# A second Strassen level for one more product of an MLP kernel, with its sums chained through ScalarE and its weights split on VectorE

## The chip, the cores and the metric

The kernel runs on one core of a Trainium2 chip. The metric is device time in microseconds (us) of that core. A run over 1.5% above the fastest of its kernel would count as slow. The engines are PE (TensorE), DVE (VectorE), ACT (ScalarE), POOL (GpSimd) and SP (SyncE, which here only issues DMAs).

## The reference

```python
x: (8, 1024, 1024)   w1: (1024, 4096)   w2: (4096, 1024)      # float32
h = x @ w1
h = 0.5 * h * (1 + np.tanh(np.sqrt(2 / np.pi) * (h + 0.044715 * h ** 3)))
return (h @ w2).astype(np.float32)
```

## The kernel before

The 8192 rows of x go through in eight superblocks of 1024 rows, SB0 to SB7. Both matmuls of a superblock use one Strassen level: seven products M1 to M7 of half-size blocks instead of eight. The first matmul works through sixteen chunks of the hidden dimension; `g` is the result after the activation, as four blocks `g["11"]` to `g["22"]` in SBUF. From SB2 on, the second matmul applies the scheme once more inside M1, M2, M3, M6 and M7 (class `Inner`, seven inner products each), and M4 and M5 are plain.

An inner product needs sums of w2's sub-blocks ("splits"), which are made once from w2's blocks (the "raw pieces", loaded from DRAM), written to DRAM and loaded again in every superblock. The splits of M1 and M3 are made on GpSimd in SB2's first matmul. At the end of every first matmul from SB2 on, GpSimd also makes four differences of g's sub-blocks in advance (`EARLY`).

```python
# in matmul1, for each chunk c of 16; product() is 4 matmuls of 512 columns on PE; banks from 8 of PSUM
product(pb, w, 4, True, False);  v = temp();  nc.scalar.copy(out=v, in_=pb)
product(qb, w, 5, True, False);  u = temp();  tt(u, v, qb, SUB)      # SBUF tensor and PSUM bank
...                                                                 # four more tt of that kind
if sb == 2 and c < 8 and c % 2 == 0:
    split_on_pool(FROM_SUMS[c // 4], c // 2 % 2)                    # GpSimd: w2 splits of M1, M3
...
if sb > 1 and c >= NI - 4:                                          # GpSimd: the early differences
    m, b = EARLY[c - NI + 4]
    early[m][b] = unit(NI // 2, HT // 2)
    gu, gv = (inner_block(g[t], b) for t in A_TERMS[m])
    nc.gpsimd.tensor_tensor(out=early[m][b], in0=gu, in1=gv, op=SUB)

# matmul2: Inner.steps, cut; three PSUM banks, evacuated by ScalarE twice and by VectorE otherwise
self.multiply(1, ab, True);   v = temp(); act_copy(v, ab)
self.multiply(6, bb, True);   tt(c12, pair(v), pair(bb), ADD, True)
self.multiply(2, ab, False);  act_copy(c11, pair(ab))
...
```

`tt` is a `tensor_tensor` on VectorE, `unit` a 4 KB-per-partition buffer from a pool of 26, `True` as its last argument pins its place in the engine's order. Such a pinned operation holds up everything behind it in VectorE's queue (in the changed kernel, behind a pair of splits that takes 9.73 us from 483.97, the next sum starts at 493.62, though PE had stopped at 487.64).

## Time and profile before

| | before |
|---|---|
| median | 1527.61 us (three runs, 1527.45 to 1528.31) |
| span of the profiled run | 1525.9 us |
| PE busy | 1517.1 us, 99% |
| one first matmul | 96.8 us |
| plain product M4 or M5 | 13.81 us |
| second-level product | 12.23 us |

The head of the profile page, kernel before (busy time, share of the span, instructions):

```profile
span 1525.9 us, 22990 instructions
PE 1517.1 (99%) x8702; PEld 852.3 (56%) x8702; DVE 1073.8 (70%) x1354; ACT 486.3 (32%) x817; POOL 357.2 (23%) x380
```

PE is busy all the time, so the time is the sum of the matmuls. The timeline of PE, kernel before, SB2's second matmul (columns: start, duration, engine, line, operation, output<-input, shape, count; a bracket at the end, where there is one, gives idle time ahead and what ended it):

```profile
505.86 13.98 PE L791 MATMUL ps<-u,g 128*128 128x512 f16 x64
519.67 1.91 PE L726 MATMUL ps<-u 128*128 128x256 f16 x16
...
556.36 13.98 PE L791 MATMUL ps<-u,gc 128*128 128x512 f16 x64
570.17 1.91 PE L726 MATMUL ps<-u,g 128*128 128x256 f16 x16
```

M4 runs from 505.86 to 519.67, M5 from 556.36 to 570.17: 13.81 us each. M1, M2 and M3 fill the 36.69 us between 519.67 and 556.36, 12.23 us each. No line has a bracket: nothing waits.

In the opening, VectorE makes sums of two SBUF tensors (`u<-u`, 128x2048 f16) while GpSimd casts weights. The timelines of VectorE and of GpSimd, kernel before:

```profile
114.39 1.22 DVE L142 TENSOR_TENSOR u<-u 128x2048 f16<-128x2048 f16 x1
116.12 0.68 DVE L142 TENSOR_TENSOR tmp<-tmp,ps 128x512 f32<-128x512 f32 x1
116.72 1.85 DVE L142 TENSOR_TENSOR u<-u 128x2048 f16<-128x2048 f16 x1
```

```profile
114.93 2.56 POOL L161 CAST u<-gc 128x1024 f16<-128x1024 f32 x2 [3.07 <-PE ps L366]
```

The same operation takes 1.22 us at 114.39, where it starts ahead of the casts, and 1.85 us at 116.72, where a cast of GpSimd, the second of the pair, still runs until 117.49. The first cast of the pair, which started behind VectorE's operation at 114.39, was held in its turn: it lasted 1.57 us, where most of the 30 casts of this shape in the trace last 1.04. The operation with a PSUM operand keeps its 0.68 us beside a cast.

### The profile page before, as it was taken

The page shows a single profiled execution, that of the slowest core. Times are in us where ns is not written, and L with a number is a line of the kernel's source. Part 1 is how long each engine was busy: PE and PEld are TensorE (multiplying, and loading weights), DVE is VectorE, ACT ScalarE, POOL GpSimd, SP SyncE. Part 2 cuts the span into 40 slices and gives each one's busy share as a digit, 9 for nine tenths or more (in the row PEclk, how much of TensorE's full clock was granted, in tenths as well). Part 3 has the DMA queues.
Part 4 walks back from the last instruction along what each step waited for, and adds up shares of the span by engine and source line. Part 5 has one row for each costly group of instructions (what it writes and reads, how often), then busy time and mean ns, then how long its engine had stood idle before and what let it go on. Part 6 is the DMA issues. An engine that isn't in the chain of part 4 may idle for free.

```text
span 1525.9 us, 22990 instructions
## 1 busy us (share of the span) xinstructions
PE 1517.1 (99%) x8702; PEld 852.3 (56%) x8702; DVE 1073.8 (70%) x1354; ACT 486.3 (32%) x817; POOL 357.2 (23%) x380
## 2 busy tenths in 40 slices
PE   9999999999999999999999999999999999999999
PEld 4444444444444677446764477544875448744486
DVE  5876868768755787557875587656876567855786
ACT  6655024410144212442124411344113441144300
POOL 1242011211297022130212203131121400204011
PEclk9999999999999999999999999999999999999999
DMA  9999985894998899769996699966999769993697
GB/s 317 348 327 349 253 281 184 281 304 156 351 362 232 309 324 312 240 159 328 321 305 212 176 348 320 312 186 198 329 308 325 185 211 320 306 353 90 221 326 185
DMA packets 226191, 417.84 MB, mean 274 GB/s; under 512 B 78752, under 2 KB 85920, under 8 KB 225184
## 3 DMA queue, kind: packets, MB, share of 16 engines
q1 hardware_dynamic: 193536, 314.64, 61.4%
q0 software_dynamic: 32544, 101.73, 24.4%
q8 instruction: 68, 1.11, 0.3%
q14 instruction: 43, 0.35, 0.1%
HBM read 311.43 MB, written 119.54 MB: 282 GB/s over the span
## 4 chain that ended last, share of the span: by engine, by line
PE 85%; DVE 0%; issue 0%
PE ps L366 44%; PE ps L726 24%; PE ps L791 17%; DVE u L142 0%
## 5 line engine op out<-in xcount | busy, mean ns | idle before, releaser
L366 PE MATMUL ps<-u 128*128 128x512 f16 x3584 | 776.1, 379 | 3.6 <-DVE tmp L142 1.5
L366 PEld LDWEIGHTS <-u 128*128 128x128 f16 x3584 | 350.5, 98 | 427.1 <-issue 4.7
L142 DVE TENSOR_TENSOR tmp<-tmp,ps 128x512 f32<-128x512 f32 x528 | 361.7, 686 | 298.1 <-ACT tmp L430 114.6
L376 ACT ACTIVATE g<-tmp 128x512 f16<-128x512 f32 x256 | 161.1, 630 | 294.4 <-DVE tmp L142 294.3
L726 PE MATMUL ps<-u,gc 128*128 128x256 f16 x1920 | 224.3, 273 | 0.0
L142 DVE TENSOR_TENSOR u<-u 128x2048 f16<-128x2048 f16 (+3 forms) x233 | 211.9, 937 | 16.6 <-ACT u L321 11.7
L791 PE MATMUL ps<-u,gc 128*128 128x512 f16 x1024 | 222.6, 379 | 0.0
L726 PEld LDWEIGHTS <-gc 128*128 128x128 f16 x1920 | 187.9, 98 | 21.7
L376 ACT ACTIVATE g<-ps 128x512 f16<-128x512 f32 x256 | 151.4, 596 | 88.1 <-PE ps L366 87.9
L791 PEld LDWEIGHTS <-gc 128*128 128x128 f16 x1024 | 100.1, 98 | 119.6
L791 PE MATMUL ps<-u,g 128*128 128x512 f16 x640 | 139.8, 379 | 0.0
L490 POOL DMA_DIRECT2D out_dram<-u x58 | 58.5, 1019 | 311.2 <-DVE u L142 299.0
L142 DVE TENSOR_TENSOR u<-u,ps 128x512 f32<-128x512 f32 x131 | 89.7, 685 | 46.1 <-PE ps L791 17.0
L158 ACT COPY tmp<-ps 128x512 f32<-128x512 f32 x54 | 31.6, 585 | 272.1 <-PE ps L726 161.3
L469 POOL TENSOR_TENSOR u<-g,g 128x2048 f16<-128x2048 f16 x24 | 97.2, 4067 | 75.0 <-ACT g L376 60.1
L791 PEld LDWEIGHTS <-g 128*128 128x128 f16 x640 | 62.7, 98 | 75.5
L726 PE MATMUL ps<-u,g 128*128 128x256 f16 x864 | 103.1, 273 | 0.0
L478 POOL DMA_DIRECT2D out_dram<-u x52 | 39.0, 770 | 249.0 <-ACT u L158 227.3
L430 ACT COPY tmp<-ps 128x512 f32<-128x512 f32 x128 | 72.9, 569 | 69.7 <-PE ps L366 69.7
L142 DVE TENSOR_TENSOR tmp<-ps,tmp 128x512 f32<-128x512 f32 x128 | 88.3, 690 | 5.9 <-PE ps L366 1.2
L726 PEld LDWEIGHTS <-g 128*128 128x128 f16 x864 | 84.5, 98 | 11.1
L142 DVE TENSOR_TENSOR u<-tmp,ps 128x512 f32<-128x512 f32 x60 | 41.3, 688 | 63.9 <-PE ps L726 41.4
(42 smaller groups left out, 736.2 us busy)
## 6 DMA issues: line engine op xcount, KB each, us to landing
u<-w_d SPq DMA_DIRECT2D x384, 256.0 KB, 7.2
u<-in_d SPq DMA_DIRECT2D x120, 512.0 KB, 7.3
u<-raw_d SPq DMA_DIRECT2D x132, 256.0 KB, 6.6
out_dram<-u POOLq DMA_DIRECT2D x58, 512.0 KB, 9.0
u<-raw_d SPq DMA_DIRECT2D x56, 512.0 KB, 7.1
gc<-in_w_dram SPq DMA_DIRECT2D x48, 512.0 KB, 6.5
w_d<-u POOLq DMA_DIRECT2D x36, 512.0 KB, 4.2
raw_d<-u SPq DMA_DIRECT2D x32, 512.0 KB, 9.9
```

The costliest lines, as they stand in the source:

```text
L142: i = nc.vector.tensor_tensor(out=out, in0=in0, in1=in1, op=op)
L158: tc.keep_in_program_order(nc.scalar.copy(out=out, in_=in_))
L366: nc.tensor.matmul(bank, lhsT=ops[:, k, :], rhs=xs[m][:, k, :], start=(first and k == 0), stop=(k == KH - 1), skip_group_check=not first,)
L376: gelu_last[0] = nc.scalar.activation(out=g[b][:, c, :], in_=src, func=GELU)
L430: nc.scalar.copy(out=v, in_=pb)
L469: nc.gpsimd.tensor_tensor(out=early[m][b], in0=gu, in1=gv, op=SUB)
L478: return nc.gpsimd.dma_start(out=out2[r0:r0 + P, o0:o0 + OH], in_=src, **kw)
L490: return nc.gpsimd.dma_start(out=rows, in_=src, **kw)
L726: tc.keep_in_program_order(nc.tensor.matmul(bank[:, i * OH // 2:(i + 1) * OH // 2], lhsT=t[:, c, i * P:(i + 1) * P], rhs=self.y[j][:, c, : ...
L791: i = nc.tensor.matmul(pair(bank), lhsT=a[:, c, :], rhs=chunks(pieces[c // QC])[:, :, c % QC, :], start=(first and c == 0), stop=(c == NI ...
```

## The change

Its intent: give M5 the second level too (1.58 us less of PE time in each of SB2 to SB7), let one PSUM bank keep accumulating through four of the seven inner products while ScalarE copies its running value out, which relieves VectorE, and make M5's w2 splits in SB2's first matmul beside those of M1 and M3. M1's stay on GpSimd; M3's and M5's go to VectorE, two operations each in chunks 5 to 12. GpSimd's early differences become six.

```diff
-FROM_SUMS = (1, 3)
-INNER = MADE_INNER + FROM_2 + FROM_SUMS
+IN_M1 = {0: (1, 0), 1: (1, 1), 2: (5, 0), 3: (3, 0), 5: (3, 1), 7: (5, 1)}
+INNER = MADE_INNER + FROM_2 + (1, 3, 5)
-EARLY = ((1, "11"), (1, "21"), (2, "11"), (2, "21"))
-W_ORDER = (1, 6, 2, 7, 5, 4, 3)
+EARLY = ((1, "11"), (1, "21"), (2, "11"), (2, "21"), (6, "11"), (6, "21"))
+W_ORDER = (1, 2, 6, 5, 7, 3, 4)
 ...
-            if sb == 2 and c < 8 and c % 2 == 0:
-                split_on_pool(FROM_SUMS[c // 4], c // 2 % 2)
+            if sb == 2:
+                if c in IN_M1:
+                    jobs = split_in_m1(*IN_M1[c])
+                    while jobs and c < 2:
+                        jobs.pop(0)()                    # M1: on GpSimd, at once
+                    splits += jobs
+                for _ in range(2 if 4 < c < 13 else 0):
+                    splits.pop(0)()                      # M3, M5: on VectorE, pinned
 ...
+            if sb == 2 and c == NI - len(EARLY):
+                mark = nc.gpsimd.tensor_copy(out=pace, in_=g["11"][:, c, :2])
-            if sb > 1 and c >= NI - 4:
+            if sb > 1 and c >= NI - len(EARLY):
 ...                                                     # in Inner.steps, a is kept accumulating:
+            for n, (j, bank, first, out, adds) in enumerate((
+                (1, a, True, "11", ()),
+                (2, b, True, None, ("11",)),
+                (6, a, False, "12", ()),
+                (5, c, True, None, ("12",)),
+                (7, a, False, "22", (("22", c),)),
+                (3, b, True, None, ("12",)),
+                (4, a, False, "21", ()),
+            ), 1):
+                self.multiply(j, bank, first)
+                if out is not None:
+                    t = quarter(into, out)
+                    if self.base is None:
+                        act_copy(t, pair(bank))
 ...                                                     # load(): the two result halves ("into") of a
+            into = dict(zip((2, 5), into))               # product are taken from the pool of units
+                if j in into:                            # after its second and its fourth weight tile
+                    into[j]()
```

(Cut: `W_SUMS` and the job table of the second matmul are rewritten, the next superblock's x differences partly go in place.)

## The prediction

> **What bounds the kernel now.** TensorE. The profile's first part gives PE 1517.1 of 1525.9 us (99%) busy; in the timeline nothing waits after the first 45 us, and PE's waits sum to under 5 us. Granted clock 0.999. So time is the sum of matmuls. From differences of starts in the timeline (busy spans overlap): a plain product of the second matmul (64 matmuls of 512 columns) takes 13.81 us, 215.8 ns each; a second-level product (7 x 16 matmuls of 256 columns) 12.23 us, 109.2 ns each. [...]
>
> **Removed.** M5's 64 wide matmuls become 112 narrow ones in six superblocks (SB2 to SB7): 13.81 - 12.23 = 1.58 us each, 9.5 us in all (0.62%), all on the critical path if nothing new stalls PE. Also gone: M5's accumulating store into block 12.
>
> **Added.**
> - VectorE, per superblock: M5's differences and sums (8 of 1.22 us) replace 4 of 1.22; more f32 adds of 0.685 us to fold M5 in; one evacuating add less in each inner product (ScalarE copies instead, 0.585 us); two differences move to GpSimd (4.07 us each, late in the first matmul). Second matmul before: about 41 x 1.22 + 41 x 0.685 = 78 of 88.7 us; after: 43 x 1.22 + 44 x 0.685 = 82.6 of 87.2 us, 95%. I estimate M6 overbooked (14 us in 12.2), a lag of about 3 us that the next stage absorbs.
> - DMA, per superblock: 1.5 MB more w2 loads, 1 MB fewer stores. The windows by stage show DMA share 0.95 to 1.08 and 253 to 374 GB/s, so it is near full; but by the order of SP's queue loads are free to issue at least 14 us before use (18 before the change), against 7 to 8 us to landing.
> - PSUM: the bank that keeps accumulating must be copied by ScalarE (0.585 us) while one other 16-matmul product (1.75 us) runs: fits.
> - SB2 only: 4 MB more traffic in a first matmul at 0.92 DMA share (340 to 409 GB/s early), with a quiet stretch (103 to 142 GB/s, 481 to 493 us) to absorb it; 16 VectorE operations of 0.72 us in slots where VectorE is busy 3.4 of 6 us. Fits.
> - SB7: M7 evacuates by VectorE, behind M6's lag: I estimate 0.5 to 1 us of PE wait, once.
>
> **Predicted.** 1527.6 - 9.5 + about 1 = 1519.0 us; 80% range 1517.4 to 1522.5. Faster by over 2%: 0.01; within 2%: 0.97; slower by over 2%: 0.02.
>
> **What would show it.** Right: PE 99% and continuous; M5's stage 12.2 instead of 13.8 us, a superblock 183.9 instead of 185.5; SB2's first matmul still 97 us; 288 more matmuls; VectorE over 90% in the second matmul; DMA share about 1.0 in M3, which had 253 GB/s. Wrong: PE idle at M6 or M7 released by a DMA (all 26 buffers used) or by VectorE (lag over 4 us, last sums late); PE idle at the third or fifth product inside an inner product, released by ScalarE.
>
> **What would make it wrong.** Sustained DMA saturation from M3 to M7, with loads landing after 14 us rather than 8: some us per superblock, which would eat the gain. VectorE's lag compounding (its waits for banks and the four sum buffers leave no slack). In SB2, raw pieces landing late would block VectorE's in-order queue, and with it the first matmul.

## The result, and the profile after

Slower: 1550.41 us median (1549.01 to 1552.05, four runs) against 1527.96 (1527.45 to 1528.82), ratio 1.0147 (95% interval 1.0129 to 1.0164). A ratio is the mean time of one kernel's fast runs over that of the other's of the same rounds, so it is not quite the ratio of the medians quoted.

The head of the page and two of its groups, kernel after (a group's columns: line, engine, operation, output<-input, shape, count | busy us, mean ns of one | idle us just before them, and what ended most of it):

```profile
span 1548.7 us, 23813 instructions
PE 1515.2 (98%) x8990; PEld 881.3 (57%) x8990; DVE 1127.1 (73%) x1400; ACT 520.1 (34%) x874; POOL 370.2 (24%) x359
...
L367 PE MATMUL ps<-u 128*128 128x512 f16 x3584 | 782.0, 381 | 19.8 <-DVE tmp L143 18.3
...
L750 PE MATMUL ps<-u,gc 128*128 128x256 f16 x2304 | 257.5, 273 | 7.7 <-ACT u L159 7.5
```

There are 288 more matmuls, as intended, but PE now waits: 18.3 us in the first matmuls for VectorE (16.8 of them in SB2's), and 7.5 us in second-level products for ScalarE. Where, the timeline of PE tells, kernel after:

```profile
450.89 1.02 PE L367 MATMUL ps<-u 128*128 128x512 f16 x4 [1.26 <-DVE tmp L143]
...
494.35 8.76 PE L367 MATMUL ps<-u 128*128 128x512 f16 x28 [6.71 <-DVE tmp L143]
511.43 17.39 PE L367 MATMUL ps<-u 128*128 128x512 f16 x68 [8.32 <-DVE tmp L143]
...
752.61 3.66 PE L750 MATMUL ps<-u,g 128*128 128x256 f16 x32
756.94 7.15 PE L750 MATMUL ps<-u,gc 128*128 128x256 f16 x64 [0.67 <-ACT u L159]
...
765.67 3.66 PE L750 MATMUL ps<-u 128*128 128x256 f16 x32
770.16 7.15 PE L750 MATMUL ps<-u,gc 128*128 128x256 f16 x64 [0.84 <-ACT u L159]
```

The first three lines are SB2's first matmul, the last four M3 and M5 of SB3. The windows of two stages, kernel after: SB2's first matmul, then SB3's M1 to M7 without M4 (columns: window, length, then for PE, PEld, DVE, ACT and POOL busy us and instructions, granted clock of PE, DMA share, GB/s):

```profile
409.27:528.65 119.38, 102.60 (x449) 45.04 (x448) 88.20 (x100) 45.49 (x78) 61.64 (x55) 0.93 0.88 282
...
728.16:803.35 75.19, 73.68 (x674) 65.74 (x672) 62.97 (x76) 14.07 (x24) 9.84 (x11) 1.00 0.96 301
```

And the same two in the kernel before, SB2's first matmul and M1 to M7 without M4 of SB3:

```profile
409.04:505.86 96.82, 96.82 (x449) 43.82 (x448) 57.35 (x84) 45.70 (x78) 65.55 (x52) 1.00 0.92 298
...
705.13:780.07 74.94, 74.94 (x625) 61.08 (x624) 59.85 (x71) 8.79 (x15) 14.59 (x18) 1.00 1.02 321
```

So there are two losses.

- **SB2's first matmul** takes 119.4 us, and 96.8 before: 22.6 us more.
- **Each of SB2 to SB6** should save 1.58 us in the second matmul. SB3's goes from 74.94 to 75.19 us, because M3 takes 13.06 and M5 13.22 us instead of 12.23: 0.83 + 0.99, about 1.83 us lost (the run bufs below was forecast with 1.84). SB7 has neither wait.

The sum: -6 x 1.58 + 22.6 + 5 x 1.83 = +22.3 us. Measured, the medians differ by 22.45 us.

What VectorE and GpSimd did in SB2's last chunks, the timelines of VectorE and of GpSimd, kernel after:

```profile
477.92 1.29 DVE L143 TENSOR_TENSOR u<-u 128x1024 f16<-128x1024 f16 x2
...
483.97 9.73 DVE L143 TENSOR_TENSOR gc<-gc 128x1024 f16<-128x1024 f16 x2
...
498.56 12.22 DVE L143 TENSOR_TENSOR gc<-gc 128x1024 f16<-128x1024 f16 x2
```

```profile
484.35 8.06 POOL L479 TENSOR_TENSOR u<-g,g 128x2048 f16<-128x2048 f16 x2
...
497.55 4.07 POOL L479 TENSOR_TENSOR u<-g,g 128x2048 f16<-128x2048 f16 x1
501.56 8.05 POOL L479 TENSOR_TENSOR g<-g,g 128x2048 f16<-128x2048 f16 x2
```

The two splits of chunk 10 took 1.29 us together. Those of chunk 11 took 9.73 us, and those of chunk 12 12.22 us, and each pair ends just after GpSimd's early differences end (484.35 + 8.06 = 492.41, VectorE 493.70; 501.56 + 8.05 = 509.61, VectorE 510.78). The trace counts VectorE as busy all the while, so no wait is listed for these splits. Behind them in VectorE's queue stand the sums that free PSUM's banks, and PE stops.

PE also loses more than it waits for. The windows around the wait of 6.71 us, kernel after (the last three columns are granted clock, DMA share, GB/s):

```profile
490.00:493.00 3.00, 0.00 (x0) 0.00 (x0) 2.97 (x1) 0.00 (x0) 2.41 (x1) 0.96 1.33 262
493.00:496.00 3.00, 1.65 (x4) 0.55 (x4) 2.48 (x4) 1.07 (x2) 0.00 (x0) 0.50 0.57 126
496.00:499.00 3.00, 3.00 (x9) 1.03 (x8) 1.73 (x3) 0.97 (x3) 2.55 (x3) 0.50 0.72 199
```

After the idle time the granted clock is 0.50, and matmuls start 0.427 us apart instead of 0.216: about seven in 3 us where fourteen start at full clock (a window also counts those that only reach into it). In this trace the clock fell 5.1 and 3.3 us after PE had stopped, and came back 5.2 us after PE had started again, both times. (Shorter waits, in two runs below, differ: in the run both one of 1.90 us, with one of 0.17 after it, was followed by a clock of 0.50 in the window 454 to 456 us; four waits in M4 of the run later, 1.76 us the longest, were not, with 1.00 in the windows from 505 to 514 us.) SB2's first matmul lost 22.6 us, with 16.8 us of waits; of the rest, 5.8 us, about 5.1 is this clock (26 matmuls in all that started later than at full clock).

### The profile page after: what moved, and what is told of

Its sections match the earlier page's. It is cut to its first block, busy times and chain, and to the rows that moved or that the text cites. A ratio compares the mean times of both kernels' runs of the same rounds, so it can differ in the third digit from the quotient of the medians.

```text
span 1548.7 us, 23813 instructions
## 1 busy us (share of the span) xinstructions
PE 1515.2 (98%) x8990; PEld 881.3 (57%) x8990; DVE 1127.1 (73%) x1400; ACT 520.1 (34%) x874; POOL 370.2 (24%) x359
## 4 chain that ended last, share of the span: by engine, by line
PE 82%; DVE 2%; issue 1%; ACT 0%; DVEq 0%; ACTq 0%
PE ps L367 43%; PE ps L750 28%; PE ps L801 12%; DVE gc L143 1%; DVE u L143 1%; ACT u L159 0%; DVE g L143 0%; DVE tmp L143 0%; DVEq L143 0%; ACTq L159 0%
## 5 line engine op out<-in xcount | busy, mean ns | idle before, releaser
L367 PE MATMUL ps<-u 128*128 128x512 f16 x3584 | 782.0, 381 | 19.8 <-DVE tmp L143 18.3
L367 PEld LDWEIGHTS <-u 128*128 128x128 f16 x3584 | 351.9, 98 | 447.8 <-issue 28.7
L750 PE MATMUL ps<-u,gc 128*128 128x256 f16 x2304 | 257.5, 273 | 7.7 <-ACT u L159 7.5
L143 DVE TENSOR_TENSOR u<-u 128x512 f32<-128x512 f32 (+3 forms) x286 | 245.6, 892 | 16.4 <-ACT u L322 12.5
L159 ACT COPY u<-ps 128x512 f32<-128x512 f32 x164 | 96.1, 586 | 419.2 <-PE ps L750 300.4
L500 POOL DMA_DIRECT2D out_dram<-u x68 | 66.6, 1177 | 404.1 <-DVE u L143 355.5
L143 DVE TENSOR_TENSOR u<-u,ps 128x512 f32<-128x512 f32 x164 | 111.9, 682 | 41.0 <-PE ps L801 16.1
L801 PE MATMUL ps<-u,gc 128*128 128x512 f16 x640 | 138.8, 379 | 0.0
L750 PE MATMUL ps<-u 128*128 128x256 f16 x864 | 99.2, 273 | 0.0
L750 PEld LDWEIGHTS <-u 128*128 128x128 f16 x864 | 84.5, 98 | 11.1
L143 DVE TENSOR_TENSOR u<-g,g 128x2048 f16<-128x2048 f16 x48 | 57.5, 1220 | 44.2 <-PE ps L750 40.0
```

The costliest lines, as they stand in the source:

```text
L143: i = nc.vector.tensor_tensor(out=out, in0=in0, in1=in1, op=op)
L159: tc.keep_in_program_order(nc.scalar.copy(out=out, in_=in_))
L367: nc.tensor.matmul(bank, lhsT=ops[:, k, :], rhs=xs[m][:, k, :], start=(first and k == 0), stop=(k == KH - 1), skip_group_check=not first,)
L500: return nc.gpsimd.dma_start(out=rows, in_=src, **kw)
L750: tc.keep_in_program_order(nc.tensor.matmul(bank[:, i * OH // 2:(i + 1) * OH // 2], lhsT=t[:, c, i * P:(i + 1) * P], rhs=self.y[j][:, c, : ...
L801: i = nc.tensor.matmul(pair(bank), lhsT=a[:, c, :], rhs=chunks(pieces[c // QC])[:, :, c % QC, :], start=(first and c == 0), stop=(c == NI ...
```

## The experiments

Theory 1 for the first loss: VectorE's splits read two SBUF tensors, and such an operation cannot run while GpSimd runs one of its own, but waits (the lock, below). VectorE's sums in the first matmul read one SBUF tensor and one PSUM bank and are free of it. The trace before fits both halves (1.85 instead of 1.22 us, and 0.68 us kept, beside a cast); port, lock and free test them. Rivals: GpSimd only shares bandwidth; the slots are too full for VectorE; the raw pieces come late by DMA.

Theory B for the second loss: ScalarE's copy waits for its target buffer, not for its input. In the built program's addresses, the target of the first copy of M3 (`into[3]`) has the slot that M3's own second weight tile leaves, so it can't be written before the second inner product is done. That of M5 has the slot of M2's result, which VectorE is still adding up. Building the kernel again and matching its instructions with the trace confirms both: in SB3 the last matmul that reads that weight tile ends at 756.27 and the copy starts at 756.31; VectorE's last addition on M2's result ends at 769.45 and the copy starts at 769.53. Rival: ScalarE or VectorE is late by itself.

### port: the lock by itself

A kernel of its own (it returns zeros). Its output is wrong, which doesn't matter for the time. Each phase is meant to start both engines together:

```python
def v_two16(): nc.vector.tensor_tensor(out=vo, in0=va, in1=vb, op=SUB)   # 128x1024 f16, two SBUF tensors
def v_psum():  nc.vector.tensor_tensor(out=fo, in0=fa, in1=ps, op=SUB)   # 128x512 f32, SBUF and PSUM
def v_copy32(): nc.vector.tensor_copy(out=fo, in_=fa)                    # 128x512 f32, one SBUF tensor
def g_two():   nc.gpsimd.tensor_tensor(out=go, in0=ga, in1=gb, op=SUB)   # 128x2048 f16
def g_dma():   nc.gpsimd.dma_start(out=out2[r:r + P, :], in_=zero)
phase(v_two16, 6, None, 0);  phase(v_two16, 6, g_two, 3);  phase(v_psum, 8, g_two, 3)
...                                              # two-input f32, and one-input copies, f16 and f32
phase(v_two16, 6, g_copy, 3);  phase(v_two16, 12, g_dma, 6)
```

> The disputed cost by itself; the result is zeros on purpose, so wrong. Phases: VectorE operations of one kind, alone or while GpSimd runs three tensor_tensor of 128x2048 f16 back to back (about 12 us). Theory 1 (a VectorE operation that reads two SBUF tensors cannot run while GpSimd runs one, and waits, counted as busy, until GpSimd is done): two-input f16 operations take 0.68 us alone, but the one that meets GpSimd lasts until GpSimd's last of the three ends (8 us or more); those that read one SBUF tensor and PSUM keep 0.69 us. Theory 2 (GpSimd merely shares bandwidth): all of them longer by some tens of per cent, none by many us. Theory 3 (the long operations of the changed kernel waited for late DMA data or buffers): nothing is longer here, since no DMA is in these phases. For two-input f32, for one-input copies and for GpSimd issuing DMAs I have no firm expectation; they are measured to learn.

Measured, the timelines of VectorE and then of GpSimd, run port:

```profile
7.26 4.32 DVE L119 TENSOR_TENSOR vo<-va,vb 128x1024 f16<-128x1024 f16 x6
...
11.96 15.63 DVE L119 TENSOR_TENSOR vo<-va,vb 128x1024 f16<-128x1024 f16 x6
...
31.88 5.73 DVE L125 TENSOR_TENSOR fo<-fa,ps 128x512 f32<-128x512 f32 x8
...
75.11 10.17 DVE L131 COPY fo<-fa 128x512 f32<-128x512 f32 x6
...
95.28 8.68 DVE L119 TENSOR_TENSOR vo<-va,vb 128x1024 f16<-128x1024 f16 x12
```

```profile
11.90 12.97 POOL L134 TENSOR_TENSOR go<-ga,gb 128x2048 f16<-128x2048 f16 x3
...
27.89 12.33 POOL L134 TENSOR_TENSOR go<-ga,gb 128x2048 f16<-128x2048 f16 x3
...
95.11 3.33 POOL L141 DMA_DIRECT2D out_dram<-zero  x6
```

Six two-input operations take 4.32 us alone (0.72 each) and 15.63 us beside three of GpSimd: one by one, the first three lasted 4.55, 4.42 and 4.42 us, the next three 0.69. Eight operations with a PSUM operand ran beside the second and third of GpSimd's (32.02 to 40.22 us) at 0.69 us each; the first of the three had already held a small copy of VectorE that prepares the phase (3.99 us). GpSimd issuing DMAs held nothing up here: twelve take 8.68 us (0.72 each). A one-input copy between SBUF tensors was held too (0.43 us alone, 4.15 beside GpSimd). Theory 1 stands in its main point, and bandwidth sharing falls. Late data falls as a necessary cause, since no operand here comes by DMA. (My text said that no DMA is in these phases. The writing of the zeros to DRAM in fact ran beside them until about 78 us, and the first and the third phase were none the longer for it. Between 85 and 95 us, where the DMA share is 0.00, a two-input operation beside a one-input copy of GpSimd still took 2.26 us instead of 0.69.) One part of what I expected was off: each waiting operation got in after one operation of GpSimd, not after all three. Here GpSimd left a gap of 0.08 us between its operations; in the changed kernel they followed without one, and a split waited for two or three of them. The gap is not shown to be what decides: in the run lock below GpSimd left none, and VectorE got in after one (2.08 and 4.42 us for the pair at 655.06).

### apart, bufs, both: each cause taken away, and the two together

apart keeps VectorE's splits as they are and moves GpSimd's work in SB2:

```diff
-            if sb == 2 and c == NI - len(EARLY):
-                mark = nc.gpsimd.tensor_copy(out=pace, in_=g["11"][:, c, :2])
 ...                                   # cut: other superblocks keep one difference a chunk from chunk 10
+            if sb == 2:
+                if c == 13:
+                    mark = nc.gpsimd.tensor_copy(out=pace, in_=g["11"][:, c, :2])
+                pick = {13: EARLY[:1], 14: EARLY[1:2], 15: EARLY[2:4]}.get(c, ())
 ...                                   # cut: M6's two in SB2, by VectorE in M4
```

> The changed kernel, with one thing moved in SB2: GpSimd's early differences start after chunk 13 (not 10), after VectorE's last w2 split, and are four (not six; the two of M6 are made by VectorE in M4 as in the kernel before). VectorE's splits stay as they are. Theory 1 (lockout by GpSimd): SB2's first matmul falls from 119.4 to 97 to 99 us, no split over 2 us but the one in chunk 5 that meets the end of GpSimd's M1 splits; time 1550.4 - 21 = about 1529 to 1531. Rival (slots too full for VectorE, or raw pieces late by DMA): the splits in chunks 11 and 12 still stall, time stays about 1548 to 1551.

bufs is one line:

```diff
-    up = ctx.enter_context(tc.tile_pool(name="up", bufs=26))
-    tp = ctx.enter_context(tc.tile_pool(name="tp", bufs=10))
+    up = ctx.enter_context(tc.tile_pool(name="up", bufs=27))
+    tp = ctx.enter_context(tc.tile_pool(name="tp", bufs=9))
```

> The changed kernel with 27 instead of 26 buffers in the pool of units (and 9 instead of 10 of temporaries, to make room). In SB2 to SB6 the changed kernel loses 1.84 us at the third product of M3 and of M5, where PE waits for ScalarE's copy. Theory B (the copy waits for its target: the slot that the pool gave it still holds M3's own second weight tile, or M2's sums): with 27 buffers the copy runs 1.75 us sooner, a steady superblock falls from 185.7 to about 183.9 us, time 1550.4 - 5 x 1.84 = 1541.2, SB2's first matmul still 119. Rival (ScalarE or VectorE is late by itself): no change, 1550.

both has the two edits.

> Both edits: what the prediction had expected of the change. If the two causes are all there is: 1527.9 - 9.5 = about 1518.4 plus up to 2 us, and so 0.6% under the kernel before. If something else holds it, above 1522.

Measured, all correct, three rounds beside the kernel before (1528.44 us):

| run | median | ratio to before | SB2's first matmul | a steady superblock |
|---|---|---|---|---|
| changed kernel (its own rounds) | 1550.41 | 1.0147 | 119.4 | 185.7 |
| apart | 1531.9 (1527.92 to 1532.68) | 1.0023 | 97.2 | 185.7 |
| bufs | 1542.15 (1539.91 to 1544.18) | 1.0088 | 117.7 | 183.87 |
| both | 1522.7 (1521.49 to 1523.24) | 0.996 | 100.8 | 183.87 |

The two columns on the right are from the profiled runs. In apart the two splits that had lasted 9.73 and 12.22 us last 1.41 and 1.29, timeline of VectorE:

```profile
481.60 1.41 DVE L143 TENSOR_TENSOR gc<-gc 128x1024 f16<-128x1024 f16 x2
487.64 1.29 DVE L143 TENSOR_TENSOR gc<-gc 128x1024 f16<-128x1024 f16 x2
```

They stand in the same slots, with the same raw pieces from DRAM, so neither the slots nor the DMA were the cause. In bufs the copy in M3 comes when its bank is done. The timeline of ScalarE around the first copy of SB3's M3, first in the kernel after (where M3 begins at 752.61), then in bufs (where it begins at 749.17); the first line of each is the last copy of M2, and the third line of the first is M5's first copy (M5 begins at 765.67):

```profile
752.81 0.59 ACT L159 COPY u<-ps 128x512 f32<-128x512 f32 x1 [2.91 <-PE ps L750]
756.31 0.59 ACT L159 COPY u<-ps 128x512 f32<-128x512 f32 x1 [2.91 <-PE ps L750]
...
769.53 0.59 ACT L159 COPY u<-ps 128x512 f32<-128x512 f32 x1 [3.07 <-DVE u L143]
```

```profile
749.37 0.59 ACT L159 COPY u<-ps 128x512 f32<-128x512 f32 x1 [2.91 <-PE ps L750]
751.12 0.59 ACT L159 COPY u<-ps 128x512 f32<-128x512 f32 x1 [1.16 <-PE ps L750]
```

M3's first copy (756.31 and 751.12) comes 3.70 us after M3's beginning in the first, when two inner products are done, and 1.95 us in the second, when one is. M5's comes 3.86 us after M5's beginning in the first, released by VectorE, and also 1.95 us in bufs. PE's waits for ScalarE are gone in bufs, and a superblock takes the 183.9 us that the prediction gave it.

But apart came out 0.9 us over its range, and both, at 1522.7, just past the 1522 from which its expectation said that something else holds it. In both, SB2's first matmul is 100.8 us, and the timeline shows why, VectorE and then GpSimd, run both:

```profile
446.08 4.93 DVE L143 TENSOR_TENSOR gc<-gc 128x1024 f16<-128x1024 f16 x2
```

```profile
443.05 4.21 POOL L684 TENSOR_TENSOR u<-u 128x1024 f16<-128x1024 f16 x2
...
448.31 2.13 POOL L684 TENSOR_TENSOR u<-u 128x1024 f16<-128x1024 f16 x1
```

It is the same lock in chunk 5: VectorE's first two splits meet the last of GpSimd's splits of M1. In the profiled run of apart GpSimd's had begun 4.65 us earlier (424.83 instead of 429.48, to where they had waited for raw pieces in both), met less, and PE did not wait; the other three runs of apart were 4 us slower than that one. That this is why is inferred, they have no profile.

### lock and free: the lock put into the kernel before, and a control

To see whether the lock is enough by itself, without the change, the kernel before got eight operations of no use in each first matmul of SB3 to SB7, in chunks 8 to 11, where GpSimd makes its early differences. Each run has one of the two `tt` lines below, so they differ in the operands and their type alone:

```diff
             late = (c, w, qb, s2)
+            if sb > 2 and 7 < c < 12:
+                for _ in range(2):
+                    tt(scr, g["11"][:, :2, :], g["22"][:, :2, :], SUB, True)      # lock
+                    tt(scr, u, rb, SUB, True)                                     # free: rb is a PSUM bank
```

> The kernel before, with eight operations of no use in each first matmul of SB3 to SB7: in chunks 8 to 11 two VectorE subtractions of two SBUF tensors each (128x1024 f16, 0.68 us alone), while GpSimd makes its four early differences (4.07 us each). Result stays right. Lockout theory: in each of the five superblocks VectorE is held by GpSimd for up to 16 us, and since PSUM's eight banks hold less than three chunks, PE waits: 5 to 14 us a superblock, time 1528 + 25 to 70. Rival (the load of 1.4 us a chunk is what hurts, whatever is read): the same as the run free, about 1528.

> The control of the run lock: the same eight operations in the same places with the same busy time (128x512 f32, 0.69 us), but the second operand is read from PSUM. Lockout theory: no operation is longer than 0.70 us, PE does not wait, time within 1 us of the kernel before. Rival (VectorE's load): it slows as the run lock does.

Measured: lock 1558.21 us (1555.89 to 1559.18), ratio 1.0191; free 1529.01 us (1528.26 to 1530.62), ratio 1.0006, interval 0.9994 to 1.0019; the kernel before 1528.06. The same pair of operations in SB3, timeline of VectorE, run lock and then run free:

```profile
655.06 6.54 DVE L142 TENSOR_TENSOR scr<-g,g 128x1024 f16<-128x1024 f16 x2
```

```profile
657.68 1.40 DVE L142 TENSOR_TENSOR scr<-tmp,ps 128x512 f32<-128x512 f32 x2
```

Operations of equal duration in equal places cost 30 us or 1 us, according to where the second operand lies. (The type is not what matters: in port two SBUF operands of f32 were held as well, for 4.42 us.) The load on VectorE is not the cause. In lock PE waits 3.6 to 4.9 us in each of the five superblocks, less than the 5 to 14 expected, and each takes 5.8 to 7.1 us more; the rest is mostly a clock of 0.50 afterwards, again (in SB3 from 662 to 668 us).

### later, six, defer: towards a version without the stalls

later moves the first splits past GpSimd's splits of M1, to chunks 6 to 12, and M5's second raw load from chunk 7 to 8:

```diff
-                for _ in range(2 if 4 < c < 13 else 0):
+                for _ in range({6: 2, 7: 2, 8: 3, 9: 3, 10: 2, 11: 2, 12: 2}.get(c, 0)):
-IN_M1 = {0: (1, 0), 1: (1, 1), 2: (5, 0), 3: (3, 0), 5: (3, 1), 7: (5, 1)}
+IN_M1 = {0: (1, 0), 1: (1, 1), 2: (5, 0), 3: (3, 0), 5: (3, 1), 8: (5, 1)}
```

> The kernel of the run both, with VectorE's sixteen w2 splits of SB2 in chunks 6 to 12 (2, 2, 3, 3, 2, 2, 2) instead of 5 to 12 (2 each), so that the first comes after GpSimd's splits of M1, which ended at about 450 us there and held a split of chunk 5 for some 3.6 us. The second raw pieces of M5 are loaded in chunk 8 instead of 7, since their buffers come free later. Lockout theory: SB2's first matmul falls from 100.8 to 97.0 to 97.5 us, time about 1522.7 - 3.5 = 1519.2 (1518 to 1520.5). Rival (VectorE's slots are too full as such, in any chunk): three splits in a chunk would make it worse, 1523 or more.

Measured: 1521.81 us (1520.6 to 1526.66), ratio 0.9965. SB2's first matmul has no wait any more, and three splits in a chunk do no harm, so the lock was read correctly. But M4 of SB2 now waits 2.5 us in all for its own weights, which M4 of both had not waited for; that was not expected, and the time missed the range given.

six puts M5's first four splits into chunk 6 and leaves its loads where both had them:

```diff
-                for _ in range(2 if 4 < c < 13 else 0):
+                for _ in range(4 if c == 6 else 2 if 6 < c < 13 else 0):
```

defer is six with four transposing DMAs of the next x issued after the loads of M4 and M1 in SP's queue:

```diff
-                if c > 8 and c % 2:
+                if c > 8 and c % 2 and (sb, c) != (2, 15):
 ...                                              # in matmul2, after M4's and M1's loads
+            if m == 4 and sb == 2:
+                nxt.rest()                           # the transposes of chunk 15
```

> The kernel of the run both, with M5's first four splits all in chunk 6 (none in 5), the rest two each in chunks 7 to 12 as there, so that M5's second raw pieces load as early as in both. Lockout theory: no split over 1 us, SB2's first matmul 97 us. In the run later M4 of SB2 then waited 2.5 us for its w2 pieces, which SP issued behind twelve transposes at 503.6 us; here they should go out at about 502, so M4 waits 1 to 3 us: time 1520 to 1522. If that DMA wait was only the late raw load's doing, 1518.5 to 1519.5.

> The kernel of the run six, with the last four of the sixteen transposes of SB2's first matmul (for the next superblock's x) issued after the loads of M4 and M1 instead of before. If SP's queue order is what made M4's pieces late, they go out about 5 us sooner, M4 does not wait, and the time is 1527.9 - 9.5 = 1518.4 up to 1519.5. If the DMA engines as such are full, M4 or M1 waits all the same: 1520 to 1522.

Measured: six 1522.97 us (1521.12 to 1527.2), ratio 0.996; its profiled run is the slowest of its five, and M4 waits 5.4 us there (1 to 3 were expected, and 1520 to 1522 us). defer 1520.0 us (1518.76 to 1521.28), ratio 0.9944 (0.9931 to 0.9956). SP's queue, timeline of SP, six and then defer:

```profile
486.99 20.36 SPq L156 DMA_TRANSPOSE u<-xb  x12
507.45 1.97 SPq L270 DMA_DIRECT2D u<-w_d  x4
```

```profile
483.70 10.64 SPq L156 DMA_TRANSPOSE u<-xb  x8
494.44 2.97 SPq L270 DMA_DIRECT2D u<-w_d  x4
```

M4's weight pieces (the second line of each) go out 13 us sooner (5 were expected), and M4 does not wait. So it was the order of SP's queue, not the DMA engines as such. The time alone would not tell: 1520.0 us is 0.5 over the forecast and at the edge of the rival's 1520 to 1522; the profile decides. The head of defer's page shows PE at work all the time again:

```profile
span 1516.4 us, 23816 instructions
PE 1507.3 (99%) x8990; PEld 880.4 (58%) x8990; DVE 1110.8 (73%) x1402; ACT 519.8 (34%) x874; POOL 362.8 (24%) x357
```

Its span is 9.5 us under that of the kernel before, about 6 x 1.58; by the medians of the same rounds (1528.56 before) the gain is 8.6 us. defer beats both kernels, by 0.56% and by 2.0% (1520.0 against 1550.41, in different rounds).

## Why the prediction was wrong

The measured 1550.41 us lies far outside the 1517.4 to 1522.5 given; the class, within 2% of the kernel before, was right, but only because it is wide: 0.6% faster was forecast, and 1.5% slower was measured.

- **Right: what bounds the kernel, and what is removed.** 288 more matmuls; once the stalls are gone (bufs, both, defer) a steady superblock takes 183.87 us, where 183.9 was predicted, and the whole saving is 9.5 us in defer's profile (8.6 by medians).
- **Wrong, and decisive: "16 VectorE operations of 0.72 us in slots where VectorE is busy 3.4 of 6 us. Fits."** The duration was taken from operations that ran while GpSimd was quiet, and the slots were counted as if engines did not meet. Beside GpSimd's early differences two of them lasted 9.0 and 11.6 us (the first of each of the two pairs shown). SB2's first matmul took 119.4 us instead of the 97 predicted. apart (97.2 us), and lock against free, show the cause. The trace before had shown it at a small scale (1.85 instead of 1.22 us beside a cast).
- **Wrong: "the bank that keeps accumulating must be copied by ScalarE (0.585 us) while one other 16-matmul product (1.75 us) runs: fits."** The copy takes 0.59 us as said, but its target was not free: 1.83 us lost in each of SB2 to SB6, more than the 1.58 us gained. The text named the 26 buffers as a danger for weight loads, and ScalarE as a possible releaser, and did not put the two together. bufs shows it.
- **Not what happened, though named: DMA saturation and late raw pieces.** DMA share in SB3's M3 was 0.99 as predicted, but it had been 0.99 there before too, so that sign told nothing; PE did not wait for a weight load in SB2 to SB7 of the changed kernel. A late load did appear once the larger stall was out of the way (2.5 us in later, 5.4 us in the profiled run of six).
- **Sizes off, without effect.** VectorE in SB3's second matmul was busy 75.2 of 89.0 us, 84.5%, not the 95% estimated and not over 90%: back to back its operations advance faster than their single durations (0.60 us from start to start where one lasts 0.68, in SB3's M5). PE's wait in SB7 was 0.17 us, not 0.5 to 1, though M7 there took 12.84 us, 0.45 more than before.

Left open: how much of apart's excess over its best run comes from chunk 5, since only that best run has a profile; and what decides who waits, and for how many operations. By the recorded starts VectorE's split at 483.97 us was 0.38 us ahead of GpSimd's operation at 484.35 and still lasted 9.0 us; in the kernel before, VectorE's sum at 114.39 was ahead of the cast too, and there the sum kept its 1.22 us and the cast took 1.57 instead of 1.04.

## What to carry to other kernels

Before moving an operation to VectorE, look where its operands lie and what GpSimd does at that time: in these runs an operation with two SBUF operands beside one of GpSimd waited for the rest of that operation (4.4 us in port) or even for GpSimd's whole remaining stretch (11.6 us in the changed kernel), shown as busy time and not as a wait; a copy from SBUF to SBUF was held too (4.15 us in port), while an operation with one operand in PSUM was free of it (0.69 us in port; 1.40 for two in free). When an evacuation is put on another engine, check when its target buffer comes free, not only how long it takes and when its input is ready. A stall also hides the next one: after each repair, read the waits again.
